# A fused recurrent and attention block: the gate sums by a triangular product, a group norm in small steps, and index queries for three token blocks

## The chip, the cores and the metric

The kernel runs on one core of a Trainium2 chip. The time is the device time of one execution in microseconds (us), and the median of several runs is compared. Engines are named as in the profile: PE is TensorE's matmul, PEld its weight load, DVE is VectorE, ACT is ScalarE, POOL is GpSimd, SP is SyncE, which issues most transfers.

## The reference

One sequence of 512 tokens, width 1024, fp32. A first block (a mixer that joins mLSTM and RWKV7, cross attention to a memory, a convolved gated feed-forward) is followed by a second one (sparse attention over the keys that an index picks, latent attention, memory attention, gated branches). Of this, the change touches three places:

```python
def mlstm_chunkwise(q, k, v, i_pre, f_pre):        # per head
    logi, logf = i_pre, jax.nn.log_sigmoid(f_pre)
    b = jnp.cumsum(logf, -1)                        # inside a chunk
    g = b[..., -1]                                  # at its end
    a = g[..., None] - b + logi
    ...                                             # running maximum m over the chunks
    d = jnp.where(causal, b[..., :, None] - b[..., None, :] + logi[..., None, :], -jnp.inf)

def standardize_heads(y, eps):                      # the RWKV output, 8 heads of 64
    mu = jnp.mean(y, -1, keepdims=True)
    var = jnp.mean(jnp.square(y - mu), -1, keepdims=True)
    return (y - mu) * lax.rsqrt(var + eps)

def dsa_attention(q, k, v, qi, ki, wi):             # topk = min(256, 512 // 4) = 128
    def one_block(args):                            # a block is 128 queries
        dots = jnp.einsum('bqhc,bsc->bhqs', qib, ki) * (IDX_DIM ** -0.5)
        index = jnp.einsum('bhqs,bqh->bqs', jax.nn.relu(dots), wib * (IDX_HEADS ** -0.5))
        index = jnp.where(causal[None], index, NEG)
        _, idx = lax.top_k(index, topk)
        valid = idx <= q_pos[None, :, None]
        ...
```

In the first block of 128 queries no query sees more than 128 keys, so the 128 best of them are all that it sees, whatever the index says.

## The kernel before, in words

All dense products are fp32 taken apart in two parts: weights come as 256 KB units by SP's DMA into `wraw` (seven buffers), ACT rounds the high part `whi` (L153), DVE takes the low part `wlo` (L156), and PE does three matmuls of 128x512 for each depth of 128 and block (hh·whi, hl·whi, hh·wlo; `dense_tok`, L271 to L282, `mmd`, L178). PSUM's eight banks are dealt by tag: mm and q two each (dense sums), p two, s and y one each.

The program is written as Python generators that yield after each small step. `woven` merges two of them by their yields' positions: the recurrence's steps are spread evenly between dense products, so that PE has something to do while a step's result passes through ACT and DVE. PE's order is fixed as it is written there; a scheduler orders DVE, ACT and POOL by priorities and what is ready, and each engine then works through its queue in that order. A matmul into bank p must wait until the reader of the bank's former content is done, wherever that reader stands in its engine's queue.

In time, the stages are: RWKV preparation up to 160 us; inverses of small triangular matrices (they use the products KR·BK, masked to `Gm` on DVE) woven with the mLSTM projections and `gates`, to 255; the RWKV chain with the mLSTM's chunks and the memory's keys, to 430; then output, cross attention and the feed-forward to 960; the second block to the end, 1601.

Three functions are touched. `gates` (L960) works on rows of 4 partitions x 512 tokens: the log-sigmoid of the forget gate, a scan for the running maximum (L976), a second scan that adds up inside chunks of 128 (L981), two subtractions and a copy that put three quantities into `um` (the tile `yt`), then four transposes on PE, and four tiny products that spread the chunk-end values over 128 partitions by a selection matrix `selX` (L357 to L361).

`rwkv_chain` steps through 16 half-chunks of 32 tokens: `tok` transposes the chunk's inputs, `solve` and `ops` (L803) make its small operators, `step` (L820) applies them. `ops` ends in additions of DR into `St` on DVE, which empty bank p. After each four half-chunks, `rwkv_out` (L868) norms 128 tokens: statistics and aggregation for eight heads (L877, L878), a reciprocal root, then two transposes and the gating. Its stages run at fixed places of the main loop (L844 to L866). In the mixer the merged sequence counts 95 steps (`CS`).

In the second block `cols` (L1626) projects a group of columns for all four token blocks and `evac` (L1638) copies them with their row scale; `index_cols` (L1672) does so for the index queries `qi`, woven with the memory attention (`memory`, L1765), and `index` (L1688) rotates them. Block 0 of `qi` is computed but not read.

Of the kernel before, what the change touches and what calls it, by code (L numbers as in the profile page):

```python
# [8 lines left out]
F32 = mybir.dt.float32  # L9
F32R = mybir.dt.float32r  # L10
I32 = mybir.dt.int32
AF = mybir.ActivationFunctionType
# [87 lines left out]
class Build:  # L100
# [234 lines left out]
    def masks(self, keep, pool):  # L335
# [11 lines left out]
        for q in range(2):  # L347
# [8 lines left out]

        selX = keep.tile([128, 512], F32, name="selX")  # L357
        nc.gpsimd.affine_select(out=selX[32:64], in_=self.one[32:64].to_broadcast([32, 512]),
                                pattern=[[-1, 4], [0, 128]], base=0, channel_multiplier=1,
                                compare_op=OP.is_equal, fill=0.0)  # L360
        self.sel4 = selX[32:36].rearrange("p (q c) -> p q c", q=4)  # L361
# [359 lines left out]
    def rwkv_chain(self, ch, TT, yT):  # L721
# [122 lines left out]
        z, st = yield from tok(0)  # L844
        yield from solve(0, z)
        yield from ops(z, st)
        late = iter(())
        for g in range(8):
            if g < 7:
                t = yield from tok(g + 1)  # L850
            yield from part(late, 1)
            yield from step(g, 0, z, st)
            if g < 7:
                yield from solve(g + 1, t[0])
            if g % 2:
# [5 lines left out]
            if g < 7:  # L861
                z, st = t
                yield from ops(z, st)
            if g % 2 == 0:
                yield from part(late, 1)
        yield from late  # L866

    def rwkv_out(self, y, b, yT):  # L868
# [91 lines left out]
    def gates(self, ml, gt):  # L960
# [3 lines left out]
        um, sg = R["yt"], R["sg"]  # L964
        g4 = lambda: self.tile(gt, [4, 512], "g4", 5)
        li = g4()
        lf = g4()
        self.act(li, um[32:36])
        self.act(lf, um[64:68])
        e = g4()  # L970
# [4 lines left out]
        m = g4()  # L975
        nc.vector.tensor_tensor_scan(m, lf, li, 0.0, op0=OP.add, op1=OP.max)  # L976
        rst128 = e
        nc.gpsimd.memset(rst128, 1.0)
        nc.gpsimd.memset(rst128.rearrange("p (c t) -> p c t", t=128)[:, :, 0:1], 0.0)
        bc = g4()  # L980
# [4 lines left out]
        ends = gt.tile([64, 2, 4], F32, name="ends")[32:36]  # L985
        nc.gpsimd.memset(ends, 0.0)
        nc.vector.tensor_copy(ends[:, 0, :], um[32:36, 127::128])
        nc.vector.tensor_copy(ends[:, 1, 1:4], m[:, 127:511:128])
        yield 0
        p = self.pt("q")  # L990
        for c in range(NB):
            self.tr(p[:, 128 * c:128 * c + 128], um[:, 128 * c:128 * c + 128])
        cl = ml.tile([128, 4, 3, 4], F32, name="cl")
# [5 lines left out]
        self.act(eb, p[:, 0:32].rearrange("p (h a c) -> p h a c", h=4, a=2))  # L999
# [457 lines left out]
    def rope(self, pool, x, heads, c0, half):  # L1457

        sh = [128, 4, heads, half]
        cos = self.cos[:, :, None, c0:c0 + half].to_broadcast(sh)  # L1460
        sin = self.sin[:, :, None, c0:c0 + half].to_broadcast(sh)
# [105 lines left out]
    def block2(self, main, late, xT, kept, out):  # L1567
# [3 lines left out]
        with tc.tile_pool(name="b2", bufs=1, reuse_waits=RW) as p2, xd as dram:  # L1571
# [54 lines left out]
            def cols(c0, n, nk=None, src=w, ks=KD, x=h, fill=None):  # L1626

                pss = [self.pm() for _ in range(NB)]
# [9 lines left out]
            def evac(pss, t, n, scaled=True):  # L1638
                for b in range(NB):
                    if scaled:  # L1640
# [31 lines left out]
            def index_cols():  # L1672
                yield from run(1536, 512, "qi", "s1", evac)
# [9 lines left out]
                for b in range(NB):  # L1683
                    self.act(ckv[:, b], pss[b][:, 0:288], AF.Copy, scale=r2[:, b:b + 1])
                    self.act(ki[:, b, 0], pss[b][:, 288:352], AF.Copy, scale=r2[:, b:b + 1])
                    self.act(wi[:, b], pss[b][:, 352:360], AF.Copy, scale=r2i[:, b:b + 1])

            def index():  # L1688
                qi, ki, wi = T["qi"], T["ki"], T["wi"]
                self.rope(p2, qi.rearrange("p b (h d) -> p b h d", h=8)[:, :, :, 0:16], 8, 0, 8)  # L1690
# [386 lines left out]
```

## Time and profile before

| | |
|---|---|
| median of 3 runs | 1605.58 us (1602.59 to 1607.35) |
| profiled execution | 1603.29 us |
| its span, from first to last instruction | 1601.4 us |
| mean granted clock of PE | 0.988 |
| busy share: PE, DVE, ACT, POOL | 97%, 68%, 47%, 6% |
| chain of waits: PE, DVE, ACT | 70%, 6%, 1% of the span |

The busy share counts instructions that overlap only once. A matmul's listed duration includes its way through the array: of a row of them each begins before the one ahead ends. The granted clock is given as a share of 2.4 GHz; half is the lower of the two levels. A square bracket at a row's end says how long the engine stood idle before it and what ended that.

### The profile page before, as it was taken

How to read it: one execution, taken by the hardware profiler on the slowest of the kernel's cores; microseconds unless marked ns; L12 is line 12 of the kernel's file. 1: busy time of each engine (PE TensorE's matmuls, PEld its weight loads, DVE VectorE, ACT ScalarE, POOL GpSimd, SP SyncE). 2: the span in 40 equal slices, each digit the busy share in tenths (PEclk: the TensorE clock that was granted, in tenths of full speed). 3: DMA queues.
4: the chain of work that ended last, by engine and by line, in shares of the span. 5: the costliest groups of instructions: out<-in, count | busy, mean ns of one | idle time of the engine just before them, and what ended most of it. 6: DMA issues, size and time to landing. Idle time of an engine off the chain costs nothing.

```text
span 1601.4 us, 23792 instructions
## 1 busy us (share of the span) xinstructions
PE 1558.0 (97%) x8515; PEld 1250.0 (78%) x8515; DVE 1091.9 (68%) x2540; ACT 752.2 (47%) x1470; POOL 94.0 (6%) x234
## 2 busy tenths in 40 slices
PE   7999899998999999999999999999999999999999
PEld 5777787787787878888888888888877778677787
DVE  6776697888756556534554578769998758755563
ACT  5645455565545435433432444446454445543431
POOL 7000402111000000000000001000000000000000
PEclk9999899999999999999999999999999999999999
DMA  7433122133534123333333334142322213224232
GB/s 256 143 66 86 41 60 53 41 107 99 159 95 142 47 86 92 99 93 98 96 95 95 91 98 113 50 120 74 90 64 67 66 53 92 67 60 125 59 93 86
DMA packets 209590, 144.84 MB, mean 90 GB/s; under 512 B 13492, under 2 KB 190787, under 8 KB 208960
## 3 DMA queue, kind: packets, MB, share of 16 engines
q1 hardware_dynamic: 208000, 141.66, 31.2%
q0 software_dynamic: 1280, 1.52, 0.4%
q8 instruction: 67, 1.10, 0.3%
q14 instruction: 51, 0.42, 0.1%
q10 hardware_dynamic: 192, 0.14, 0.0%
HBM read 134.90 MB, written 8.39 MB: 89 GB/s over the span
## 4 chain that ended last, share of the span: by engine, by line
PE 70%; DVE 6%; ACT 1%; issue 1%; DMA 1%; DVEq 0%; ACTq 0%
PE mm L178 29%; PE q L178 29%; PE p L186 3%; PE p L189 3%; PE y L186 3%; PE s L186 2%; DVE wlo L156 1%; PE s L189 1%; DVE lqk L156 1%; PE q L186 1%; DMA kvraw<-v_kept 0%; DVE m L1730 0%; DVE s L156 0%; DVE madd L1731 0%; PE mm L186 0%
## 5 line engine op out<-in xcount | busy, mean ns | idle before, releaser
L153 ACT ACTIVATE whi<-wraw 128x512 fp32r<-128x512 f32 (+2 forms) x472 | 292.6, 622 | 514.7 <-PE mm L178 253.8
L156 DVE TENSOR_TENSOR wlo<-wraw,whi 128x512 fp32r<-128x512 f32 (+2 forms) x472 | 319.5, 678 | 202.9 <-ACT whi L153 198.8
L178 PE MATMUL mm<-hh,whi 128*128 128x512 f32 (+1 forms) x680 | 252.9, 389 | 1.2 <-ACT hh L153 0.9
L178 PE MATMUL mm<-hh,wlo 128*128 128x512 f32 (+1 forms) x616 | 237.1, 385 | 0.0
L178 PE MATMUL mm<-hl,whi 128*128 128x512 f32 x552 | 219.3, 397 | 0.0
L178 PEld LDWEIGHTS mm<-hh,whi 128*128 128x128 f32 x680 | 124.5, 190 | 25.8 <-issue 2.7
L178 PE MATMUL q<-hl,whi 128*128 128x512 f32 x352 | 139.4, 396 | 0.0
L178 PE MATMUL q<-hh,whi 128*128 128x512 f32 x352 | 139.0, 395 | 0.0
L178 PE MATMUL q<-hh,wlo 128*128 128x512 f32 x352 | 139.0, 395 | 0.0
L178 PEld LDWEIGHTS mm<-hh,wlo 128*128 128x128 f32 x616 | 116.9, 190 | 22.1 <-issue 0.5
L178 PEld LDWEIGHTS mm<-hl,whi 128*128 128x128 f32 x552 | 105.0, 190 | 20.0 <-issue 1.4
L178 PEld LDWEIGHTS q<-hl,whi 128*128 128x128 f32 x352 | 66.4, 189 | 14.7 <-issue 1.6
L178 PEld LDWEIGHTS q<-hh,wlo 128*128 128x128 f32 x352 | 66.4, 189 | 14.3 <-issue 1.0
L178 PEld LDWEIGHTS q<-hh,whi 128*128 128x128 f32 x352 | 66.5, 189 | 14.0 <-issue 0.9
L178 PE MATMUL q<-whi,hh 128*128 128x512 f32 (+2 forms) x176 | 69.0, 394 | 0.0
L178 PE MATMUL mm<-whi,hh 128*128 128x512 f32 (+2 forms) x176 | 68.7, 392 | 0.0
L178 PE MATMUL mm<-wlo,hh 128*128 128x512 f32 (+2 forms) x160 | 61.6, 385 | 0.0
L178 PE MATMUL q<-wlo,hh 128*128 128x512 f32 (+2 forms) x160 | 61.5, 385 | 0.0
L178 PE MATMUL mm<-whi,hl 128*128 128x512 f32 (+2 forms) x144 | 55.3, 384 | 0.0
L178 PE MATMUL q<-whi,hl 128*128 128x512 f32 (+2 forms) x144 | 55.3, 384 | 0.0
L153 ACT ACTIVATE at_sm<-at_sm,at_mx 128x128 f32<-128x128 f32 (+3 forms) x64 | 35.8, 559 | 41.2 <-DVE at_mx L1538 40.8
L174 DVE SCALAR_TENSOR_TENSOR fy<-fc,vcols,fy 128x512 f32<-128x512 f32 x44 | 33.0, 751 | 8.9 <-ACT fy L153 8.2
(702 smaller groups left out, 3167.2 us busy)
## 6 DMA issues: line engine op xcount, KB each, us to landing
wraw<-in_w_in_dram SPq DMA_DIRECT2D x172, 256.0 KB, 2.8
wraw<-in_f_up_dram SPq DMA_DIRECT2D x88, 256.0 KB, 2.9
wraw<-in_f_down_dram SPq DMA_DIRECT2D x40, 256.0 KB, 2.7
wraw<-in_x_wkv_dram SPq DMA_DIRECT2D x32, 256.0 KB, 3.0
wraw<-in_w_out_dram SPq DMA_DIRECT2D x32, 256.0 KB, 2.7
wraw<-in_w_branch_dram SPq DMA_DIRECT2D x24, 256.0 KB, 2.7
wraw<-in_w_mem_kv_dram SPq DMA_DIRECT2D x16, 256.0 KB, 4.7
wraw<-in_x_wq_dram SPq DMA_DIRECT2D x16, 256.0 KB, 2.8
```

Of the source, the lines that this page charges most:

```text
L153: self.pin("a", self.nc.scalar.activation(out, in_, func, **kw))
L156: self.pin("v", self.nc.vector.tensor_tensor(out, a, b, op=op))
L174: self.pin("v", self.nc.vector.scalar_tensor_tensor(out, a, s, b, op0=op0, op1=op1))
L178: ins = self.nc.tensor.matmul(out, lhsT=a, rhs=b, start=start, stop=stop)
L186: self.pin("p", self.nc.tensor.matmul(out, lhsT=a, rhs=b, start=start, stop=stop))
L189: self.pin("p", self.nc.tensor.transpose(out, in_, self.ident if ident is None else ident))
```

## The change

**Gates.** Only the maximum's scan stays on the rows, and it writes straight into `um`. The transposes follow. The sum inside a chunk is then a product with a triangle of ones (`upto`, 128x128) on the transposed 128x16 columns, two small subtractions follow, and the chunk-end values are spread by a product with a matrix whose last row is ones (`last`). `selX` is gone; POOL builds the two matrices.

**Group norm.** `rwkv_out` yields after four heads' statistics, after eight, and after the reciprocal root. The chain's main loop is a generator of its own, and behind each third of its steps one step of the oldest unfinished norm runs.

**Index queries.** Block 0 of `qi` and `wi` is neither projected nor copied, and the rotation runs over blocks 1 to 3.

```diff
     def dense_tok(self, pss, w, x, ks, first, last, cols):
-        order = [(a, t) for a in range(n) for t in range(len(pss))]
+        order = [(a, t) for a in range(n) for t in range(len(pss)) if pss[t] is not None]
...
     def rwkv_chain
-        z, st = yield from tok(0)
-        yield from solve(0, z)
-        yield from ops(z, st)
-        late = iter(())
-        for g in range(8):
-            if g < 7:
-                t = yield from tok(g + 1)
-            yield from part(late, 1)
-            yield from step(g, 0, z, st)
-            if g < 7:
-                yield from solve(g + 1, t[0])
-            if g % 2:
-                yield from late
-            yield from step(g, 1, z, st)
-            if g % 2:
-                late = self.rwkv_out(ys[g // 2 % 2], g // 2, yT)
-                yield from part(late, 1)
...
+        lates = []
+        def main():
...
+                yield from step(g, 1, z, st)
+                if g % 2:
+                    lates.append(self.rwkv_out(ys[g // 2 % 2], g // 2, yT))
...
+        for n, at in enumerate(main()):
+            yield at
+            if n % 3 == 2 and lates and next(lates[0], "end") == "end":
+                lates.pop(0)
+        for late in lates:
+            yield from late

     def rwkv_out(self, y, b, yT):
         for h in range(8):
             nc.vector.bn_stats(st[:, h], ynv[:, h])
             nc.vector.bn_aggr(ag[:, h], st[:, h])
+            if h == 3:
+                yield 0
+        yield 0
         var = rt("gvar", (128, 8), 1)
         self.ts(var, ag[:, :, 1], 64e-5, None, OP.add)
         r = self.rsqrt(ch, var, 8)
+        yield 0
...
     def gates(self, ml, gt):
-        nc.vector.tensor_tensor_scan(m, lf, li, 0.0, op0=OP.add, op1=OP.max)
...
-        nc.vector.tensor_tensor_scan(bc, rst128, lf, 0.0, op0=OP.mult, op1=OP.add)
-        self.sub(um[32:36], bc, m)
-        self.sub(um[64:68], li, bc)
-        nc.vector.tensor_copy(um[96:100], m)
...
-        nc.vector.tensor_copy(ends[:, 0, :], um[32:36, 127::128])
-        nc.vector.tensor_copy(ends[:, 1, 1:4], m[:, 127:511:128])
+        nc.vector.tensor_tensor_scan(um[96:100], lf, li, 0.0, op0=OP.add, op1=OP.max)
+        upto = gt.tile([128, 128], F32, name="upto")
+        nc.gpsimd.affine_select(out=upto, ...)
+        last = gt.tile([128, 128], F32, name="last")
+        nc.gpsimd.affine_select(out=last, ...)
         yield 0
         p = self.pt("q")
         for c in range(NB):
             self.tr(p[:, 128 * c:128 * c + 128], um[:, 128 * c:128 * c + 128])
-        self.act(cl, p.rearrange("p (c q x) -> p c q x", c=4, q=4)[:, :, 1:4, 0:4])
+        self.act(raw, pv[:, :, 1:3, 0:4].rearrange("p c q x -> p q c x"))
+        self.act(cl[:, :, 2, :], pv[:, :, 3, 0:4])
         p = self.pt("q")
-        for hd in range(4):
-            self.mm(p[:, 8 * hd:8 * hd + 8], self.sel4[:, hd, :], ends.rearrange("p a c -> p (a c)"))
+        bc = p[:, 0:16].rearrange("p (c x) -> p c x", c=4)
+        self.mm(bc, upto, raw[:, 1])
+        self.sub(cl[:, :, 0, :], bc, cl[:, :, 2, :])
+        self.sub(cl[:, :, 1, :], raw[:, 0], bc)
+        yield 0
+        p = self.pt("q")
+        pv = p[:, 0:48].rearrange("p (c q x) -> p c q x", c=4, q=3)
+        self.mm(pv, last, cl)
...
+        self.act(ebv[:, 0], pv[:, :, 0])
+        self.act(ebv[:, 1, 1:4], pv[:, 0:3, 2])
...
             def index_cols():
-                yield from run(1536, 512, "qi", "s1", evac)
+                yield from run(1536, 512, "qi", "s1", evac, b0=1)
```

The change moves instructions on DVE and PE. First DVE's queue at the gates; `g` are the tiles of four rows, `yt` is `um`, and the `p` that `Gm` reads is the bank that PE wants next. Before:

```order
L156 TENSOR_TENSOR Gm_613<-p_1760,gmask 128x512
L174 SCALAR_TENSOR_TENSOR g_1688<-g_1688,g_1691 4x512
L156 TENSOR_TENSOR wlo_1838<-wraw_1837,whi_1839 128x512
L976 SCALAR_TENSOR_TENSOR g_1696<-g_1688,g_1687 4x512
L981 SCALAR_TENSOR_TENSOR g_1700<-g_1691,g_1688 4x512
L984 COPY yt<-g_1696 4x512
L156 TENSOR_TENSOR yt<-g_1700,g_1696 4x512
L156 TENSOR_TENSOR yt<-g_1687,g_1700 4x512
L987 COPY ends<-yt 4x4
L988 COPY ends<-g_1696 4x3
L174 SCALAR_TENSOR_TENSOR q_1730<-mc_1727,vcols_573,q_1730 128x512
L156 TENSOR_TENSOR wlo_1977<-wraw_1976,whi_1978 128x512
```

And now, up to the next two masked products:

```order
L174 SCALAR_TENSOR_TENSOR yt<-yt,g_1686 4x512
L156 TENSOR_TENSOR Gm_611<-p_1748,gmask 128x512
L973 SCALAR_TENSOR_TENSOR yt<-yt,g_1685 4x512
L156 TENSOR_TENSOR wlo_1826<-wraw_1825,whi_1827 128x512
L174 SCALAR_TENSOR_TENSOR q_1718<-mc_1715,vcols_573,q_1718 128x512
L156 TENSOR_TENSOR Gm_611<-p_1772,gmask 128x512
L174 SCALAR_TENSOR_TENSOR q_1718<-mc_1715,vcols_573,q_1718 128x512 x2
L156 TENSOR_TENSOR wlo_1970<-wraw_1969,whi_1971 128x512
L156 TENSOR_TENSOR Gm_611<-p_1799,gmask 128x512
```

Between two masked products there stood two scans, three operations on rows and two tiny copies; one scan is left.

PE's order at the same place. Before, the transposes of `um` and the four products with `selX` stand between a product of the inverses and the dense ones:

```order
L186 MATMUL p_1882<-KR_607,BK_608 64x64 x16
L189 MATMUL q_1900<-ident,yt 128x128 x4
L186 MATMUL q_1907<-ends,selX 128x8 x4
L178 MATMUL mm_1843<-hh_80,whi_1839 128x512
L178 MATMUL mm_1843<-hl_81,whi_1839 128x512
```

Now:

```order
L186 MATMUL p_1870<-KR_605,BK_606 64x64 x16
L189 MATMUL q_1888<-ident,yt 128x128 x4
L186 MATMUL q_1897<-graw,upto 128x16
L186 MATMUL q_1901<-cl,last 128x48
L178 MATMUL mm_1831<-hh_80,whi_1827 128x512
L178 MATMUL mm_1831<-hl_81,whi_1827 128x512
```

Two products stand in place of four, the first behind ACT's copy `graw` of the transposes, the second behind DVE's `cl`, and no dense product stands between them.

Last, DVE's queue in the chain at the first group norm (`gst`, `gag` are its statistics; `rs_` and `Dm` belong to the mLSTM's norm). Before, the additions into `St` stand behind the last statistics:

```order
L156 TENSOR_TENSOR rs_y_3352<-rs_y_3352,rd_3336 128x4
L878 BN_AGGR gag_3374<-gst_3373 128x2 x2
L171 TENSOR_SCALAR Dm_2946<-nt_3115,mag_3339,rs_y_3352 128x128 x4
L877 BN_STATS gst_3373<-sg 128x6 x2
L878 BN_AGGR gag_3374<-gst_3373 128x2
L156 TENSOR_TENSOR St_3152<-p_3429,DR 64x384
L878 BN_AGGR gag_3374<-gst_3373 128x2
L156 TENSOR_TENSOR St_3153<-p_3429,DR 64x384
L169 TENSOR_SCALAR gvar_3391<-gag_3374 128x8
L156 TENSOR_TENSOR sg<-sg,gag_3374 128x512
```

Now four of them stand ahead of the first:

```order
L156 TENSOR_TENSOR St_3145<-p_3366,DR 64x384
L174 SCALAR_TENSOR_TENSOR rs_y_3345<-rs_t_3347,rs_y_3345 128x4
L156 TENSOR_TENSOR St_3146<-p_3366,DR 64x384
L156 TENSOR_TENSOR rs_t_3347<-rs_y_3345 128x4
L156 TENSOR_TENSOR St_3145<-p_3395,DR 64x384
L156 TENSOR_TENSOR rs_t_3347<-rs_t_3347,rs_h_3346 128x4
L156 TENSOR_TENSOR St_3146<-p_3395,DR 64x384
L174 SCALAR_TENSOR_TENSOR rs_y_3345<-rs_t_3347,rs_y_3345 128x4
L874 BN_STATS gst_3428<-sg 128x6
```

The statistics now begin after these additions, mixed with the same steps of the mLSTM's norm, and the copies of `Z` come behind their first lot.

## Rows read from the trace of the kernel before

**Rows 1.** The page's busy times: us (share of the span) xinstructions.

```profile
PE 1558.0 (97%) x8515; PEld 1250.0 (78%) x8515; DVE 1091.9 (68%) x2540; ACT 752.2 (47%) x1470; POOL 94.0 (6%) x234
```

**Rows 2.** Windows: us; busy PE, PEld, DVE, ACT, POOL; PEclk, DMA share, GB/s.

```profile
150.00:200.00 50.00, 45.62 (x456) 37.13 (x455) 35.26 (x55) 24.88 (x46) 17.56 (x15) 0.90 0.20 48
304.00:440.00 136.00, 122.88 (x1220) 103.66 (x1219) 113.97 (x330) 73.27 (x150) 19.66 (x34) 0.97 0.38 113
1015.00:1065.00 50.00, 49.81 (x292) 41.86 (x292) 36.44 (x88) 19.80 (x52) 0.00 (x0) 1.00 0.25 77
1080.00:1240.00 160.00, 158.89 (x802) 126.00 (x801) 149.57 (x431) 86.55 (x197) 3.40 (x11) 1.00 0.28 73
```

**Rows 3.** Timeline of PE at the gates: start, us, instruction [idle before <-releaser].

```profile
177.99 1.97 PE L186 MATMUL p<-KR,BK 64*64 64x64 f32 x32 [4.29 <-DVE Gm L156]
...
185.12 1.05 PE L186 MATMUL q<-ends,selX 4*128 4x8 f32 x8
```

**Rows 4.** Timeline of DVE at the gates.

```profile
170.52 2.22 DVE L981 TENSOR_TENSOR_SCAN g<-g,g 4x512 f32<-4x512 f32 x1
172.77 1.33 DVE L984 COPY yt<-g 4x512 f32<-4x512 f32 x1
174.13 1.40 DVE L156 TENSOR_TENSOR yt<-g,g 4x512 f32<-4x512 f32 x2
...
177.16 1.28 DVE L156 TENSOR_TENSOR Gm<-p,gmask 128x512 f32<-128x512 f32 x2
```

**Rows 5.** Windows behind PE's waits; columns as in rows 2.

```profile
178.00:184.00 6.00, 6.00 (x60) 4.88 (x62) 1.79 (x4) 1.23 (x2) 0.00 (x0) 0.56 0.19 46
196.00:204.00 8.00, 8.00 (x59) 6.92 (x58) 3.56 (x13) 3.32 (x7) 3.19 (x2) 0.57 0.13 33
312.00:316.00 4.00, 2.84 (x11) 2.60 (x12) 3.77 (x13) 1.19 (x3) 1.22 (x3) 0.62 0.01 2
320.00:332.00 12.00, 9.45 (x106) 8.03 (x106) 9.16 (x19) 7.77 (x17) 1.28 (x2) 1.00 0.38 109
408.00:412.00 4.00, 4.00 (x20) 3.38 (x19) 2.12 (x4) 2.77 (x7) 0.00 (x0) 0.57 0.71 252
```

**Rows 6.** Timeline of ACT at the gates.

```profile
173.85 0.63 ACT L153 ACTIVATE xt<-bonus 128x512 f32<-128x512 f32 x1 [3.42 <-POOL w L948]
...
174.90 0.58 ACT L153 ACTIVATE vT<-mm 128x512 f32<-128x512 f32 x1
175.50 1.28 ACT L153 ACT_TABLE_LOAD   x1
176.79 0.63 ACT L153 ACTIVATE th<-q 128x512 f32<-128x512 f32 x1
...
185.23 0.21 ACT L153 ACTIVATE cl<-q 128x48 f32<-128x48 f32 x1 [1.32 <-PE q L189]
```

**Rows 7.** Timeline of POOL at the gates.

```profile
167.76 0.51 POOL L978 MEMSET g<- 4x512 f32 x1 [4.51 <-DVE g L174]
...
171.73 2.08 POOL L948 TENSOR_TENSOR w<-xt,w 32x512 fp32r<-32x512 f32 x1
```

**Rows 8.** POOL's select of 128x128 on tile causT: ns min/median/max, first and last start.

```profile
L366 POOL TENSOR_SCALAR_AFFINE_SELECT causT<-zero x1: 292/292/292, 23.4 to 23.4; 128x128 f32<-128x128 f32 x1
```

**Rows 9.** PE's waits in 304–440: line <- releaser: us, times, longest.

```profile
PE p L189 <- DVE sg L156: 3.6, 2, 2.6
PE p L189 <- DVE gvar L169: 3.1, 3, 2.1
PE p L189 <- DVE mag L1122: 2.1, 1, 2.1
```

**Rows 10.** Statistics on DVE in 304–440: count | busy us, mean ns | idle before.

```profile
L878 DVE BATCH_NORM_AGGREGATE gag<-gst 128x2 f32<-128x6 f32 x32 | 5.0, 167 | 0.0
L877 DVE BATCH_NORM_STATS2 gst<-sg 128x6 f32<-128x64 f32 x16 | 3.1, 207 | 0.0
```

**Rows 11.** The chain of waits in the second block: start, us, what.

```profile
1006.33 5.44 PE mm L178 x24
```

More of the change, by code (lines that the diff above doesn't have):

```diff
@@ L355, in masks @@
         nc.gpsimd.memset(self.hsel[64:128, 1:2], 1.0)
[L357 to L361, printed above, removed]
         zero = pool.tile([128, 128], F32, name="zero")
@@ L842, in step @@
                 yield 0
-        z, st = yield from tok(0)
-        yield from solve(0, z)
-        yield from ops(z, st)
-        late = iter(())
-        for g in range(8):
-            if g < 7:
-                t = yield from tok(g + 1)
-            yield from part(late, 1)
-            yield from step(g, 0, z, st)
-            if g < 7:
-                yield from solve(g + 1, t[0])
-            if g % 2:
-                yield from late
-            yield from step(g, 1, z, st)
-            if g % 2:
-                late = self.rwkv_out(ys[g // 2 % 2], g // 2, yT)
-                yield from part(late, 1)
[L861 to L866, printed above, removed]
+        lates = []
+        def main():
+            z, st = yield from tok(0)
+            yield from solve(0, z)
+            yield from ops(z, st)
+            for g in range(8):
+                if g < 7:
+                    t = yield from tok(g + 1)
+                yield from step(g, 0, z, st)
+                if g < 7:
+                    yield from solve(g + 1, t[0])
+                yield from step(g, 1, z, st)
+                if g % 2:
+                    lates.append(self.rwkv_out(ys[g // 2 % 2], g // 2, yT))
+                if g < 7:
+                    z, st = t
+                    yield from ops(z, st)
+        for n, at in enumerate(main()):
[4 more added lines that the diff above has]
+            yield from late
     def rwkv_out(self, y, b, yT):
@@ L962, in gates @@
         sc = 0.25 / math.sqrt(128.0)
[L964 to L967, printed above, removed]
+        um = R["yt"]
+        li, e = (self.tile(gt, [128, 512], "g4", 2)[64:68] for _ in range(2))
+        lf = um[64:68]
         self.act(li, um[32:36])
-        self.act(lf, um[64:68])
-        e = g4()
         self.act(e, lf, AF.Abs)
@@ L974, in gates @@
         self.stt(lf, lf, 0.0, e, OP.min, OP.subtract)
-        m = g4()
-        nc.vector.tensor_tensor_scan(m, lf, li, 0.0, op0=OP.add, op1=OP.max)
[L977 to L980, printed above, removed]
-        nc.vector.tensor_tensor_scan(bc, rst128, lf, 0.0, op0=OP.mult, op1=OP.add)
-        self.sub(um[32:36], bc, m)
-        self.sub(um[64:68], li, bc)
-        nc.vector.tensor_copy(um[96:100], m)
-        ends = gt.tile([64, 2, 4], F32, name="ends")[32:36]
-        nc.gpsimd.memset(ends, 0.0)
-        nc.vector.tensor_copy(ends[:, 0, :], um[32:36, 127::128])
-        nc.vector.tensor_copy(ends[:, 1, 1:4], m[:, 127:511:128])
+        nc.vector.tensor_tensor_scan(um[96:100], lf, li, 0.0, op0=OP.add, op1=OP.max)
+        upto = gt.tile([128, 128], F32, name="upto")
+        nc.gpsimd.affine_select(out=upto, in_=self.one.to_broadcast([128, 128]), pattern=[[1, 128]], base=0,
+                                channel_multiplier=-1, compare_op=OP.is_ge, fill=0.0)
+        last = gt.tile([128, 128], F32, name="last")
+        nc.gpsimd.affine_select(out=last, in_=self.one.to_broadcast([128, 128]), pattern=[[0, 128]], base=-127,
+                                channel_multiplier=1, compare_op=OP.is_equal, fill=0.0)
         yield 0
@@ L1455, in tables, with rope @@
         self.cos, self.sin = cos, sin
[L1457 to L1461, printed above, removed]
+    def rope(self, pool, x, heads, c0, half, b0=0):
+        sh = [128, NB - b0, heads, half]
+        cos = self.cos[:, b0:, None, c0:c0 + half].to_broadcast(sh)
+        sin = self.sin[:, b0:, None, c0:c0 + half].to_broadcast(sh)
         x1, x2 = x[:, :, :, 0:half], x[:, :, :, half:2 * half]
@@ L1624, in sums, with cols @@
                 self.ts(r2i, r2, 8.0 ** -0.5)
-            def cols(c0, n, nk=None, src=w, ks=KD, x=h, fill=None):
-                pss = [self.pm() for _ in range(NB)]
+            def cols(c0, n, nk=None, src=w, ks=KD, x=h, fill=None, b0=0):
+                pss = [None] * b0 + [self.pm() for _ in range(b0, NB)]
                 nk = nk or 1024 // n
@@ L1639, in evac @@
                 for b in range(NB):
+                    if pss[b] is None:
+                        continue
                     if scaled:
```

10 lines of the change are left out of this document (7 added, 3 removed).

## The prediction

> **What bounds the kernel now.** I read the line of busy times first: PE is busy for 97% of the span and DVE for 68% [rows 1]. So the time is PE's, and an edit is worth what it takes from PE's work, from PE's idle time, or from the stretches in which PE runs at half its clock. Then I read the windows of the stages that the diff touches [rows 2]: PE idles 4.4 us in 150–200 and 13.1 us in 304–440 (the RWKV chain, where DVE is busy for 114 of 136 us), but 0.2 us in 1015–1065, where the index queries are projected. In 1080–1240 (the top-k search) PE and DVE are both nearly full: 158.9 and 149.6 of 160 us. The timelines and waits then say which instruction ended PE's idle time, and the clock windows what followed.
>
> All sums are made against the profiled execution: 1603.3 us, a span of 1601.4 and 1.9 around it, which I leave as it is. The median of the runs is 1605.6, so 2.3 is added at the end.
>
> **Gates, about 175 us.** PE waits 4.29 us at 173.7 to 177.99 for the second mask product of DVE (Gm) [rows 3]. In DVE's queue that product stands behind the second scan (2.22), the copy of the maxima (1.33), two subtractions (1.40) and two tiny copies [rows 4], 5.3 us in all. All of these go, or become subtractions on 128x16 columns after PE's transposes, so Gm can be done at 172.5 instead of 177.8, and PE, which comes for it at 173.7, need not wait: −4.3. The time after the wait also shows: in 178–184 the granted clock is 0.56, that is, mostly the lower of the two levels (1.2 of 2.4 GHz); at full clock the six us of PE work would take 3.4: −2.6 [rows 5]. PE ran at 1.00 until it stood still; if it no longer stands still, the fall has no cause that I see. The eight tiny products with selX take 1.05 us [rows 3] and are replaced by one of 16 and one of 48 columns: −0.5.
>
> What is late next? First the eviction of vT on ACT. Before, it stands at 174.90, ahead of a table load (1.28) and th (0.63) [rows 6]; now it is queued behind both, and ACT gets to them only after the copy of the bonus, which waits for POOL's subtraction on w (2.08) [rows 6, 7]. POOL loses two fills (0.5 and less) and ends w at 173.2; the bonus and a weight split take 1.05 (the time from 173.85 to 174.90), then 1.28, 0.63 and vT's own 0.58: 176.7. PE arrives at 173.7 + 1.0 (half of 1.97, at full clock) + 0.7 (three products) = 175.4 to 175.5: +1.2. What stands behind that wait on PE is everything, since its order is fixed. Second, PE must now wait in line for ACT's copy of the transposed sums and DVE's subtractions between its two small products. The nearest row for the copy is 0.21 us, begun 0.04 after the transposes [rows 6]; two DVE operations of this size about 0.3. With both engines free that is 0.6, with one other instruction ahead on each (0.63 on ACT, 0.7 on DVE) 1.9. I take 0.7, near the free case, since ACT had idled 1.3 us before that copy. Building the two triangles costs POOL two selects of 0.29 [rows 8], before anyone needs them. Sum: −4.3 −2.6 −0.5 +1.2 +0.7 = **−5.5**; bounds −7.4 (no new wait) and −1.7 (the second wait at 1.9, and the clock falls all the same). The selX fill, near the program's start, is long done when it is read: 0.
>
> **Group norm in the chain.** Six waits of PE in 304–440 belong to it [rows 9]: 3.6 us (two, by name for sg), 3.1 (three, gvar), 2.1 (one, mag), together 8.8 of the 13.1 us of idle time. The releasers are not what PE needs: its next transposes go to a bank that becomes free when DVE has added the block to St, and that addition is queued behind the norm's statistics. One block's eight statistics and eight aggregations are 1.6 and 1.3 us [rows 10] (half of the one row's sum, a quarter of the other's), mixed with as much of the mLSTM's norm. In the new order four St additions come before the first of these statistics, and the statistics come in two lots of four heads. The work itself stays: DVE has the same 114 us in 136 us, so some of the delay moves to the next reader, the Z copies behind the lot (its head lot is 1.5 us and the mLSTM's share about as much). So I take half of the waits: −4.4. Of the half-clock stretches 312–316 (0.62) and 408–412 (0.57) [rows 5], which cost 1.5 and 1.7 us and both follow a wait of over 2 us, I take two thirds: −2.1. Sum **−6.5**; the bounds are −12.0 (all waits and both stretches) and +2.0 (DVE's queue is only reshuffled, one wait of 2.1 like that for mag is added). The steps issue no DMA. Since the chain's steps end some thirty products earlier, the loads of x for the next stage stand four weight loads earlier on SP; the DMA share there is 0.71 [rows 5], so I cost this at nothing; it is weights that hide it, four to seven loads ahead.
>
> **Index queries.** Block 0 loses three products on each of eight k: 24 products of 128x512. The chain of waits shows 24 of these in 5.44 us [rows 11], 0.227 each, at clock 1.00. In 1015–1065 PE has no idle time in which they could hide [rows 2], so −5.4. The scaled eviction of one block leaves ACT (19.8 of 50 us) and a quarter of six rope operations DVE (36.4): nothing on the path. Against it: the memory attention is woven between these products and now has nine in place of twelve to cover each turn of its softmax; I give back 1.0 for that. Sum **−4.5**, bounds −5.4 and 0 (all is lost when DVE's full stretch at 1080–1240 comes up).
>
> Total: −5.5 −6.5 −4.5 = −16.5, so 1586.8 for the profiled execution and **1589** against the median.
>
> **Rivals.**
> - *The gates' wait comes back under other names* (0.13): vT, the copy and the subtractions and the fall of the clock eat most of it and the saving is 1.7. For it: ACT's wait of 3.42 for POOL [rows 6] is untouched. Against: DVE is relieved of 5 us just there. −12.7: 1593.
> - *The group norm's waits only move* (0.19): the Z copies are late instead, saving 1.0. For it: DVE's 84% [rows 2]. Against: half of what PE waited for stood behind work that PE does not need. −11.0: 1594.5.
> - *More goes* (0.11): all waits and both half-clock stretches of the chain (12.0), the whole 5.4, and the stretch 196–204 at 0.57 [rows 5], 3.4, which I otherwise leave. −26.3: 1579.
> - *The index saving is swallowed* (0.07) by DVE's 149.6 of 160 us [rows 2]. For it: PE can't run ahead of the top-k. Against: PE is full there as well, and DVE can start earlier by as much. −12: 1593.5.
> - *Slower* (0.06): the norm in small steps gives PE more, shorter waits in the chain, and they hold its clock at the lower level. Work done at 1.2 GHz takes twice its time, so of each us there half is lost. The gains elsewhere (5.5, 4.5, and 4.4 of waits) are 14.4 us, so it decides from 29 us at the lower level; with 50 us, +25 −14.4 = +10.6: 1616. Against it stands a row: 320–332 has 2.55 us of idle time in 12, in waits of at most 1.0, at clock 1.00 [rows 5]. The Trainium skill speaks for this rival (TensorE: Matmul & The Clock Gate, A second HAM failure mode: psum-queue depth-cycling): frequent small idles between groups of matmuls, as banks are cycled, make the clock swing between its levels. By that rule this time would be likely; by the row it is not, and I go by the row.
> - Two or more of these losses together, or a stall that I don't see, leave it where it was (0.08).
>
> **How the numbers follow.** The forecast itself has 0.36, with 1583 to 1595 as its own range: gates −3 to −7, norm −3 to −10, index −3 to −5.4, not all at one end. The range 1576 to 1602 takes in the first four rivals and the lighter part of the last; it leaves out the slower case and most of no change. A difference below 0.3% (4.8 us) can't be told from none here. Faster: 0.36 + 0.13 + 0.19 + 0.11 + 0.07 = 0.86; within 0.3% 0.08; slower 0.06.
>
> **What would show it.** Right: no wait of over 1.5 us before the Gm-fed products near 175 and a clock of 1.00 in the six us behind; PE's waits named sg, gvar and mag in the chain below 4.4 us, and at least one of its two half-clock stretches gone; 72 products for the index queries, and the stages behind the gates, the chain and the projection ending about 5.5, 12 and 16.5 us earlier. Wrong: a wait on vT or on the new products as long as the old one, Z copies as releasers of several us in the chain, a granted clock below 0.95 over the chain, or stages after the projection that take longer by what it saved.

## The result and the profile after

The changed kernel takes 1589.28 us (median of 4 runs, 1588.84 to 1592.04), the kernel before 1604.09 (4 runs, 1600.29 to 1607.35): a ratio of 0.9906, with a 95% interval of 0.9883 to 0.9929. The forecast was 1589. It was made from a median of 1605.6 of three runs and a drop of 16.5 us; a fourth run brought that median to 1604.1, and the drop is 14.8. The span of the profiled execution fell from 1601.4 to 1587.2 us. First its line of busy times, where PE has lost 11.0 us of work or listed overlap [rows 1]:

```profile
PE 1547.0 (97%) x8487; PEld 1241.5 (78%) x8487; DVE 1088.2 (69%) x2536; ACT 751.2 (47%) x1469; POOL 93.6 (6%) x233
```

Where the 14.2 us of the span went is read by setting equal PE instructions of both traces against each other and taking the difference of their start times:

| PE reaches | after minus before, us | difference in the stretch | forecast |
|---|---|---|---|
| dense work at 40 us, behind the wait for km | +2.2 | +2.2 | 0 |
| 206, behind the gates | −2.8 | −5.0 | −5.5 |
| 307, before the first group norm | −4.8 | −2.0 | 0 |
| 500, behind the chain | −7.8 | −3.0 | −6.5 |
| 950, the second block | −8.6 | −0.8 | 0 |
| 1240, behind the index queries | −14.3 | −5.7 | −4.5 |
| the end | −14.2 | +0.1 | 0 |

The row at 307 is a step of the chain; 816 dense products stand ahead of it in place of 819, so 0.7 us of its −2.0 is work that comes later, and the chain's own share is −3.7 rather than −3.0. The stages behind the gates, the chain and the projection end 2.8, 7.8 and 14.3 us earlier, where 5.5, 12 and 16.5 were forecast.

The windows that answer to [rows 2], with the last two set 10 to 15 us earlier (columns as there):

```profile
150.00:200.00 50.00, 48.24 (x465) 38.53 (x464) 35.55 (x56) 25.53 (x48) 16.94 (x12) 0.93 0.22 54
304.00:440.00 136.00, 125.64 (x1216) 106.06 (x1215) 111.26 (x327) 74.76 (x151) 20.48 (x33) 0.99 0.38 116
1000.00:1050.00 50.00, 49.78 (x298) 42.02 (x298) 37.99 (x92) 22.93 (x59) 0.00 (x0) 1.00 0.25 74
1070.00:1225.00 155.00, 153.89 (x771) 121.71 (x771) 146.26 (x423) 83.93 (x190) 3.39 (x11) 1.00 0.27 73
```

PE's idle time in 304–440 fell from 13.1 to 10.4 us only, while the stages with the index stayed full: there the work itself is less. At the gates, PE's timeline (start, us, instruction, idle time before it) now has three short waits in place of the one of 4.29 [rows 3]:

```profile
178.43 0.66 PE L189 MATMUL q<-ident,vT 128*128 128x128 f32 x4 [0.55 <-ACT vT L153]
...
181.82 0.37 PE L186 MATMUL q<-graw,upto 128*128 128x16 f32 x2 [0.38 <-ACT cl L153]
182.69 0.39 PE L186 MATMUL q<-cl,last 128*128 128x48 f32 x2 [0.50 <-DVE cl L156]
```

The windows behind them, to be held against [rows 5], show that the clock stays at 1.00 in 178–184, where it was 0.56, and falls right after in this trace. The third row answers to 196–204, where it was 0.57:

```profile
178.00:184.00 6.00, 4.69 (x56) 3.54 (x58) 3.74 (x11) 2.66 (x11) 0.00 (x0) 1.00 0.36 87
184.00:190.00 6.00, 6.00 (x74) 4.71 (x71) 1.58 (x4) 0.20 (x2) 1.14 (x1) 0.72 0.01 3
194.00:202.00 8.00, 8.00 (x52) 6.87 (x51) 4.18 (x14) 3.41 (x6) 3.09 (x2) 0.79 0.05 6
```

And PE's waits in 304–440 (line, releaser: us, times, longest). None of the names of [rows 9] is left, but others stand there:

```profile
PE p L189 <- DVE St L156: 2.6, 2, 2.2
PE p L189 <- DVE yt L156: 2.5, 1, 2.5
PE p L186 <- DVE Z L766: 2.2, 3, 1.0
PE p L186 <- DVE Z L801: 1.9, 2, 1.1
PE p L189 <- DVE Z L766: 0.8, 1, 0.8
```

### The profile page after: what moved, and what is told of

Read it like the earlier page. It is cut to its first block, busy times and chain, and to the rows that moved or that the text cites. A ratio compares the mean times of both kernels' runs of the same rounds, so it can differ in the third digit from the quotient of the medians.

```text
span 1587.2 us, 23736 instructions
## 1 busy us (share of the span) xinstructions
PE 1547.0 (97%) x8487; PEld 1241.5 (78%) x8487; DVE 1088.2 (69%) x2536; ACT 751.2 (47%) x1469; POOL 93.6 (6%) x233
## 4 chain that ended last, share of the span: by engine, by line
PE 70%; DVE 6%; issue 1%; ACT 1%; DMA 1%; DVEq 0%; ACTq 0%
PE mm L178 30%; PE q L178 27%; PE p L186 3%; PE p L189 3%; PE y L186 3%; PE s L186 2%; DVE wlo L156 1%; PE s L189 1%; DVE lqk L156 1%; PE q L186 1%; DMA kvraw<-v_kept 1%; DVE m L1739 0%; DVE s L156 0%; DVE madd L1740 0%; PE mm L186 0%
## 5 line engine op out<-in xcount | busy, mean ns | idle before, releaser
L178 PE MATMUL mm<-hh,whi 128*128 128x512 f32 (+1 forms) x744 | 278.0, 389 | 0.0
L178 PE MATMUL mm<-hh,wlo 128*128 128x512 f32 (+1 forms) x680 | 262.3, 386 | 0.0
L178 PE MATMUL mm<-hl,whi 128*128 128x512 f32 x616 | 245.2, 398 | 0.0
L178 PEld LDWEIGHTS mm<-hl,whi 128*128 128x128 f32 x616 | 116.8, 190 | 23.2 <-issue 2.8
L178 PE MATMUL q<-hh,whi 128*128 128x512 f32 x288 | 113.7, 395 | 0.0
L178 PE MATMUL q<-hl,whi 128*128 128x512 f32 x288 | 113.1, 393 | 0.0
L178 PE MATMUL q<-hh,wlo 128*128 128x512 f32 x288 | 112.9, 392 | 0.0
L178 PEld LDWEIGHTS q<-hh,whi 128*128 128x128 f32 x288 | 54.5, 189 | 11.6 <-issue 0.7
L178 PEld LDWEIGHTS q<-hh,wlo 128*128 128x128 f32 x288 | 54.4, 189 | 11.3
L178 PEld LDWEIGHTS q<-hl,whi 128*128 128x128 f32 x288 | 54.4, 189 | 11.0 <-issue 0.2
```

The source lines that it names most:

```text
L178: ins = self.nc.tensor.matmul(out, lhsT=a, rhs=b, start=start, stop=stop)
```

## The experiments

Each kernel was run in five rounds against the kernel before; ratios are to that one, with 95% intervals. The changed kernel's own interval, 0.9883 to 0.9929, is wide, so a run on top of it says little by its ratio alone. Four questions were open: whether the parts add up, where the +2.2 us at the start came from, why the norm gave half of its term, and what the clock does.

**1. The gates alone** (`gates` and the selX fill as in the change, the rest as before).

```diff
-        nc.gpsimd.affine_select(out=selX[32:64], ...)
...
-        nc.vector.tensor_tensor_scan(bc, rst128, lf, 0.0, op0=OP.mult, op1=OP.add)
...
+        self.mm(bc, upto, raw[:, 1])
...
+        self.mm(pv, last, cl)
```

> Only the gates' part of the change on the kernel before (the selX fill is gone with it). In the trace of the whole change PE is 2.5 us later than before at 30 us (it waits 4.03 us instead of 1.85 for ACT's km) and gains 5.3 us between 173 and 204. Theory S: the later start belongs to this part, since POOL, without the selX fill (0.81 us), comes earlier to its own subtraction (lwl) and disturbs DVE's reciprocal root: km is waited for again by about 4 us, and the net is -5.3 + 2.3 = -3 us, ratio 0.998. Rival C: the late start is chance of one execution: no longer wait for km, -5.3 us, ratio 0.9967. In both: no wait for Gm near 175, three waits of together about 1.4 us (vT, graw, cl), and one stretch of some 2.7 us at half clock behind them that costs 1.3.

Measured: 0.9965 (0.9952 to 0.9977), 1599.03 us, that is −5.6 us. PE's waits at the gates are 0.55, 0.38 and 0.51, as in the changed kernel, but the half-clock stretch that was expected behind them did not come; one stands at 190–196 instead:

```profile
181.75 0.39 PE L186 MATMUL q<-cl,last 128*128 128x48 f32 x2 [0.51 <-DVE cl L156]
```

```profile
184.00:190.00 6.00, 6.00 (x63) 4.74 (x64) 3.37 (x4) 1.12 (x2) 3.60 (x2) 1.00 0.02 4
190.00:196.00 6.00, 6.00 (x59) 5.58 (x59) 1.97 (x5) 2.40 (x4) 4.64 (x3) 0.79 0.17 43
```

The wait for km is 1.67 us, not longer than before, though PE is still 1.1 us late at 40 us. Theory S's 0.998 lies outside the interval; the rival's 0.9967 lies inside.

**2. The group norm alone** (the three new yields and `main()` with a step of the norm behind each third of its own).

```diff
+        for n, at in enumerate(main()):
+            yield at
+            if n % 3 == 2 and lates and next(lates[0], "end") == "end":
...
```

> Only the group norm's part on the kernel before. Theory M (waits move): the waits for sg, gvar and mag (8.8 us) are gone, about 10 us of others stand in 304 to 440 (St, Z, the last block's yt), both half-clock stretches are gone (3.2 us), one comes at the end of the chain; net -3 us in the chain, ratio 0.998. Rival (the sum on record): -6.5, ratio 0.996. The start is as before: km waited for by about 1.9 us if theory S of the gates' run holds.

Measured: 0.9978 (0.9966 to 0.9989), 1601.54 us: −3.5 us. In its trace PE gains 4.3 us between 307 and 437 (5.0 with the 0.7 of work put off). The waits for sg, gvar and mag are gone, and 9.4 us of others for St, Z and yt stand there. The half-clock stretch that was expected at the end of the chain did not come; one stands near 331 us. Theory M holds for the waits and the size; 0.996 lies outside the interval.

**3. The index queries alone.**

```diff
...
-                yield from run(1536, 512, "qi", "s1", evac)
+                yield from run(1536, 512, "qi", "s1", evac, b0=1)
...
```

> Only the index queries for blocks 1 to 3 on the kernel before. Theory F (full price): 24 products by 0.227 us and nothing given back, -5.4 to -5.7 us, ratio 0.9965. Rival (the sum on record): -4.5, 0.9972. Rival: swallowed by DVE's full stretch behind it, 0, 1.000. The start as before.

Measured: 0.9969 (0.9958 to 0.9981), 1599.66 us: −5.0 us. The runs can't tell −4.5 from −5.4, but the trace can: PE is 1.7 us late at 1010 and 4.0 early at 1240, −5.7, as in the whole change (runs 1 and 2, without the edit, lose 0.5 and 0.7 us there). Nothing is given back to the softmax or to DVE's full stretch. The three parts come to −5.6 −3.5 −5.0 = −14.1 us, the whole change to 0.94% of 1604, −15.1: they add up within the intervals.

Its start, which should have been as before, was late (PE's timeline, the only row of its wait for km):

```profile
29.93 0.50 PE L178 MATMUL mm<-whi,m2h 128*128 128x512 f32 x1 [4.07 <-ACT km L153]
```

**4. The whole change with the fill back.**

```diff
+        selX = keep.tile([128, 512], F32, name="selX")
+        nc.gpsimd.affine_select(out=selX[32:64], in_=self.one[32:64].to_broadcast([32, 512]), ...)
```

> The whole change with the selX fill put back on POOL at its old place; nothing reads it. Theory S: km is waited for by about 1.9 us again and all that follows comes 2.3 us earlier than in the changed kernel: -16.5 us against the kernel before, ratio 0.990. Rival C (chance of one execution): no difference from the changed kernel, ratio 0.9906 to 0.9912, and the wait for km is as long in some kernels with the fill as without it.

Measured: 0.9902 (0.9882 to 0.9922), 1588.39 us; no difference from the change (0.9906). Its wait for km happened to be 1.19 us:

```profile
26.89 0.50 PE L178 MATMUL mm<-whi,m2h 128*128 128x512 f32 x1 [1.19 <-ACT km L153]
```

So the kernels with the fill have shown 1.85, 1.22, 4.07 and 1.19 us for this wait, those without it 4.03 and 1.67, and in runs 5 to 11 from 1.28 to 3.90: theory S is dead. The wait varies by up to 2.9 us from one execution to the next, and the +2.2 of the table is that.

**5. Dense products between the gates' small ones.**

```diff
         self.act(cl[:, :, 2, :], pv[:, :, 3, 0:4])
+        yield 0
         p = self.pt("q")
...
-    ... part(lstm, 12), gates, part(lstm, GS), ...
+    ... part(lstm, 12), part(gates, 1), part(lstm, 1), part(gates, 1), part(lstm, 1), gates, part(lstm, GS - 2), ...
```

> The changed kernel, with three dense products between the transposes of um and the product with upto, and three between that and the product with last. In the changed kernel PE waits 0.38 us for ACT's cl and 0.50 for DVE's cl there, and runs 2.7 us at half clock right behind (184.9 to 187.6), at a cost of 1.3. Theory W (the clock fell for these idle times): both waits and the half-clock stretch go, -2.2 us against the changed kernel, ratio to the kernel before about 0.989. Rival T (it fell for the run of small products and transposes there, which are the same): the waits go, the stretch stays, -0.9 us, 0.990.

Measured: 0.9898 (0.9881 to 0.9914), 1588.66 us: no difference that the runs can tell. In the trace both waits are gone, and 184–190 has a clock of 1.00. Another half-clock stretch stands six us later:

```profile
184.00:190.00 6.00, 5.88 (x75) 5.00 (x74) 5.32 (x9) 2.45 (x8) 4.83 (x3) 1.00 0.01 3
190.00:196.00 6.00, 6.00 (x49) 5.21 (x49) 3.38 (x8) 1.79 (x3) 3.44 (x2) 0.72 0.16 44
```

This decides nothing between the theories: runs 1, 4, 6, 7 and 8 kept both waits (0.38 and 0.50 or 0.51), and in each of them the clock stayed at 1.00 for the eight us behind as well. The stretch at 184–190 stood in the changed kernel's one trace only. Between 40 and 262 us PE gains 6.7 us on the kernel before, against 5.1 in the changed kernel and 6.2 in run 1; near 265 us 0.4 of it are lost again, where the changed kernel gained 1.2 (told of below). The runs do not confirm the gain.

**6. The chain's steps wider.**

```diff
-PS, LS, CS, XS = 16, 75, 95, 188
+PS, LS, CS, XS = 16, 75, 80, 188
```

> The changed kernel with the chain's steps set wider (80 in place of 95 per unit of the woven sequence). The norm's steps no longer count as steps, so the main steps stand 105/88 closer among the dense products than before; 80 gives them their former distance. Theory P (the density of the chain's steps on DVE causes the waits that are left, 10.3 us in the chain): they fall to about 6, -3 to -4 us against the changed kernel, ratio to the kernel before about 0.988. Rival D (what stands ahead in DVE's queue at each norm causes them, whatever the distance): the same 10 us, the chain ends later with fewer dense products behind it, 0 to +2 us, 0.9906 to 0.992.

Measured: 0.9882 (0.9866 to 0.9897), 1586.55 us. PE's waits in 304–440 (as above), where the long ones for St and yt are down to 0.6 and 0.4:

```profile
PE mm L178 <- DVE hh L156: 1.2, 1, 1.2
PE p L186 <- DVE Z L766: 1.1, 3, 0.4
...
PE p L189 <- DVE St L156: 0.6, 2, 0.4
...
PE p L189 <- DVE yt L156: 0.4, 1, 0.4
```

All of them come to 7.5 us, against 10.2 in the changed kernel. That is for theory P, with a smaller step than it gave. Two things go against a simple reading. At 80 the steps do not have their former distance but a wider one: between the first and the last products of St with Z stand dense products worth 261 of 512 columns before, 237 in the changed kernel and 282 here. And the chain has a longer half-clock stretch, near 309 to 319 us (windows of the changed kernel and of this run):

```profile
308.00:324.00 16.00, 14.54 (x177) 11.94 (x174) 15.48 (x54) 9.01 (x19) 1.95 (x5) 1.00 0.33 96
```

```profile
304.00:440.00 136.00, 128.49 (x1205) 107.92 (x1206) 112.60 (x306) 77.68 (x156) 18.44 (x33) 0.96 0.38 115
308.00:324.00 16.00, 14.28 (x137) 13.18 (x138) 12.24 (x33) 8.12 (x18) 0.52 (x2) 0.68 0.40 116
```

The loss of 5.1 us (16 times 0.32) stands at the same place in runs 9 and 10, which also have 80. What causes it was not tested.

**7. No reciprocal root in the group norm** (the variance is the factor; this part of the computation is left out).

```diff
-        r = self.rsqrt(ch, var, 8)
+        r = var
```

> The changed kernel without the reciprocal root of the RWKV group norm: the variance itself is the factor, so twelve small DVE operations per norm, which follow one another and take 3 us in all with what comes between, are left out. Theory D (PE's remaining waits stand behind this chain on DVE): the wait for St (2.18) and the last one for yt (2.47, with its half-clock stretch of 1.7) shrink by most of their length, -3 to -5 us against the changed kernel, ratio about 0.988. Theory P (density of steps): DVE loses 2 of 111 us there and the waits stay within 1 us of 10.3; 0 to -1, 0.990.

Measured: 0.9875 (0.9858 to 0.9892), 1585.80 us. The wait for yt is gone, St's longest is 1.5, and between 307 and 437 PE gains 9.2 us on the kernel before instead of 3.0. Of these 6.2 us 3.4 are idle time and 1.7 the half-clock stretch. The longest waits in 304–440:

```profile
PE p L186 <- DVE Z L766: 2.2, 3, 1.0
PE p L189 <- DVE St L156: 1.9, 3, 1.5
PE p L189 <- DVE Z L766: 1.2, 1, 1.2
PE p L186 <- DVE Z L801: 0.7, 1, 0.7
```

For yt theory D holds. In the changed kernel DVE ends the root with the first of these rows, only then makes yt, and PE stands still for it:

```profile
418.70 0.17 DVE L174 SCALAR_TENSOR_TENSOR rs_y<-rs_t,rs_y 128x8 f32<-128x8 f32 x1
418.90 0.69 DVE L156 TENSOR_TENSOR yt<-yt,rs_y 128x512 f32<-128x512 f32 x1
```

```profile
419.64 0.66 PE L189 MATMUL p<-ident,yt 128*128 128x128 f32 x4 [2.47 <-DVE yt L156]
```

For the other waits the run doesn't separate the theories. Theory P's number was worked out with 2 us less work on DVE; in the changed kernel's trace the four roots' 48 operations have 7.4 us of DVE's time, so leaving them out also makes its queue less dense.

**8. The norm's two wide operations on POOL.**

```diff
-        self.sub(ynv, ynv, ag[:, :, 0:1].to_broadcast([128, 8, 64]))
-        self.mul(ynv, ynv, r[:, :, None].to_broadcast([128, 8, 64]))
+        nc.gpsimd.tensor_tensor(ynv, ynv, ag[:, :, 0:1].to_broadcast([128, 8, 64]), op=OP.subtract)
+        nc.gpsimd.tensor_tensor(ynv, ynv, r[:, :, None].to_broadcast([128, 8, 64]), op=OP.mult)
```

> The changed kernel with the group norm's subtraction and multiplication (two operations of 128x512 per norm, 0.68 us each on DVE) moved to POOL, which is busy for 20 of 136 us there. Theory D: DVE's queue is shorter by 1.36 us at each norm and the waits for St and Z fall by 2 to 3 us in all, though the last norm's yt comes later (POOL took 1.3 to 2.1 us for such an operation near 170): -1 to -2 us, ratio about 0.990. Rival X (POOL's operations hold up DVE's while they run, as far as the trace lets one think so): DVE's own operations there get longer and nothing is gained, 0 to +3 us, 0.991 to 0.9925.

Measured: 0.9880 (0.9865 to 0.9894), 1585.65 us. In the trace St's waits fall to 1.2 us, and the last norm's rises:

```profile
PE p L189 <- POOL yt L884: 3.3, 1, 3.3
...
PE p L189 <- DVE St L156: 1.2, 3, 0.7
```

Its chain gains only 0.3 us on the changed kernel. The rest of its trace's lead lies where the instructions are the same: 0.9 at the start, 1.3 at the gates and 1.5 in the clock near 265 (below). So the ratio is no evidence for POOL. What rival X names is seen too: three short operations of DVE, which mostly take 0.15 to 0.17 us, took 0.89 to 1.02 beside POOL's and ended within 0.03 us of them. The first of them, and the same one in the changed kernel:

```profile
311.07 1.05 POOL L883 TENSOR_TENSOR sg<-sg,gag 128x512 f32<-128x512 f32 x1 [5.96 <-DVE gag L875]
```

```profile
311.14 1.01 DVE L212 TENSOR_SCALAR rs_i<-gvar 128x8 int32<-128x8 int32 x1
```

```profile
316.11 0.15 DVE L212 TENSOR_SCALAR rs_i<-gvar 128x8 int32<-128x8 int32 x1
```

**9 to 11. The pieces together**, all on one chip: 9 has the spread products and the wider steps (edits 5 and 6), 10 has in addition POOL for the first three norms, 11 is 10 with the steps at 95 again.

```diff
+        eng = nc.vector if b == 3 else nc.gpsimd
+        eng.tensor_tensor(ynv, ynv, ag[:, :, 0:1].to_broadcast([128, 8, 64]), op=OP.subtract)
+        eng.tensor_tensor(ynv, ynv, r[:, :, None].to_broadcast([128, 8, 64]), op=OP.mult)
```

> The changed kernel with both the dense products between the gates' small ones and the chain's steps at 80. If the two gains add (0.9 us of waits and the half-clock stretch behind them; about 2.4 us in the chain), some 4 us less than the changed kernel, ratio to the kernel before about 0.987. If the gates' gain is given back, as in the run with it alone, by the half-clock stretch near 265 us that comes and goes between executions with the same waits, the ratio is that of the steps at 80 alone, 0.988.

> The same, with the group norm's subtraction and multiplication on POOL for the first three of the four norms, and on DVE for the last, for which PE waited 3.29 us when POOL did them. Theory D (DVE's queue): the St wait is under 1 us, the last yt wait under 0.5; another -1 to -2 us, ratio about 0.986. Rival (the wider steps have taken these waits already): no difference from the run without POOL, 0.987.

> As the one before, but with the chain's steps at 95 again. Theory D: St's wait falls from 2.18 to 0.7, yt's stays at 2.5 with its half-clock stretch, -1 to -2 us against the changed kernel with the spread products, ratio about 0.9885. If the distance of the steps is what counts, it is over 2 us slower than with 80.

| | median of runs | ratio |
|---|---|---|
| 9, spread, steps at 80 | 1585.78 (1583.98 to 1586.30) | 0.9887 (0.9874 to 0.9901) |
| 10, and POOL for three norms | 1585.93 (1583.51 to 1586.56) | 0.9888 (0.9874 to 0.9901) |
| 11, spread, POOL, steps at 95 | 1589.17 (1588.35 to 1590.56) | 0.9909 (0.9895 to 0.9923) |

The distance of the steps is worth 3.2 us (10 against 11, whose runs do not overlap). POOL adds nothing: 10 equals 9, though its waits for St and yt are down to 0.2 and 0.3 us, and with the steps at 95, 11 (0.9909) is no faster than run 5 (0.9898). Against the rounds of 6, the spread products add nothing either; run 9's rival gave the number, but not the reason, since its trace has a clock of 1.00 near 265. So the best version found is the change with its steps at 80, 17 to 19 us below the kernel before (runs 9 and 6).

**The clock near 265.** In the kernels with the steps at 95 the chain's first steps have the same three waits there. Before, and in run 4 (PE's timeline):

```profile
263.51 1.08 PE L186 MATMUL p<-rgu,TT 32*32 32x128 f32 x32 [0.88 <-ACT whi L153]
266.71 0.38 PE L186 MATMUL p<-St,Z 32*64 32x96 f32 x4 [0.91 <-ACT Z L153]
267.35 0.70 PE L186 MATMUL p<-St,Z 32*64 32x96 f32 x10 [0.26 <-DVE Z L807]
```

```profile
255.48 1.08 PE L186 MATMUL p<-rgu,TT 32*32 32x128 f32 x32 [0.91 <-ACT whi L153]
258.69 0.38 PE L186 MATMUL p<-St,Z 32*64 32x96 f32 x4 [0.93 <-ACT Z L153]
259.32 0.70 PE L186 MATMUL p<-St,Z 32*64 32x96 f32 x10 [0.26 <-DVE Z L806]
```

The eight us that begin six us after the first of these rows (windows; the clock is the third number from the end), of before, of the changed kernel and of run 4:

```profile
269.51:277.51 8.00, 7.80 (x43) 6.17 (x40) 3.18 (x8) 3.01 (x6) 2.15 (x5) 0.63 0.02 4
```

```profile
266.62:274.62 8.00, 7.48 (x59) 5.89 (x59) 4.03 (x9) 3.56 (x7) 2.16 (x5) 0.79 0.13 30
```

```profile
261.48:269.48 8.00, 7.47 (x80) 5.89 (x77) 4.88 (x11) 4.19 (x8) 2.16 (x5) 1.00 0.13 33
```

The same waits, and a clock of 0.63, 0.79 or 1.00: in the eight us that is from 3.0 us to nothing. In runs 2 and 3 it was 0.63 and 0.65, in 5 and 7 0.68 and 0.70, in 11 0.79, in 1 and 8 1.00; in 6, 9 and 10, which have their steps elsewhere, 1.00. The three kernels with the old gates lie at 0.63 to 0.65. Those with the new ones spread from 0.68 to 1.00, and of these the changed kernel and runs 4, 7 and 8 have the same instructions up to there but for one fill. What decides it was not settled.

## Why the prediction was right

The time came out as forecast, in part by luck: the drop was 14.8 us where 16.5 was forecast, and the median of the kernel before came out 1.5 us lower than the one it was reckoned from. Of the three terms two had about the right size, and the third was about half.

**What bounds the kernel.** Right: what came off PE's work (index) showed in full, and what came off its idle time (gates) nearly so.

**Gates, −5.5.** Right in the mechanism, and in the sum: −5.0 in the trace, −5.6 alone (−6.1 in that trace). Gm was no longer waited for. The two new waits were 0.55 for vT, where I had 1.2, and 0.38 + 0.50 for the small products, where I had 0.7. The clock's part was right by luck in this trace. It fell anyway for a while behind the small products: 0.72 in 184–190 costs 1.7 us (6 times 0.28), against 2.6 in 178–184 before. And the stretch 196–204, which I had left alone, gave up to 1.7 us of its 3.4 (0.79 in 194–202 now). The first is no price of the new waits, since in five runs with the same waits the clock stayed at 1.00 behind them.

The queue ahead of Gm was perhaps not all of the gates' own making. Its two scans of 4x512 took 2.36 and 2.22 us while POOL worked on `rgl`, `x` and `w` (168.2 to 173.8 [rows 7]). At 65 us in the same trace, with POOL idle, a scan of 128x512 took about half of that (DVE's timeline of before):

```profile
64.85 1.23 DVE L619 TENSOR_TENSOR_SCAN rt<-rst,rt 128x512 f32<-128x512 f32 x1
```

No run moved POOL's work away from there, so whether that alone would have shortened the wait stays open.

**Group norm, −6.5.** The step that failed is "so I take half of the waits: −4.4" with "two thirds" of the half-clock stretches, −2.1. The six waits of 8.8 us did all go, but the idle time of the chain fell by 2.7 us only (13.1 to 10.4), since waits for St, yt and Z of 10.0 us took their place (these names had 1.8 before). Both half-clock stretches went too in this trace, and a new one came behind the wait for yt (window of the changed kernel):

```profile
420.00:424.00 4.00, 4.00 (x15) 3.25 (x14) 1.84 (x3) 2.62 (x6) 0.00 (x0) 0.57 0.30 73
```

It costs 1.7 us, so the clock's part was −1.5. Together that is −4.2; the trace shows −3.7 with the 0.7 us of work put off, the run of this part alone −3.5. The clock's part is a matter of one execution: in run 4, whose chain has the same instructions and the same waits, the clock over the chain is 0.96, no better than the 0.97 before:

```profile
304.00:440.00 136.00, 126.86 (x1193) 107.84 (x1194) 107.66 (x304) 74.63 (x150) 18.31 (x28) 0.96 0.39 117
```

The prediction's sentence that "some of the delay moves to the next reader" was right, and its amount too small: the sign named there as wrong, "Z copies as releasers of several us", did come, with 4.9 us. The mechanism that I did not weigh is that the norm's steps no longer count in the woven sequence. I saw that the chain would end some thirty products earlier, but asked only what that does to the loads. The main steps then stand closer among the dense products (237 in place of 261, run 6), DVE's queue gets denser, and the root's dependent operations stand ahead of yt. Runs 10 and 11 show the first by their times, run 6 by its waits; run 7 shows the second for yt. How the wait for St divides between the two stays open. The rival "the waits only move" had the better mechanism; its size (−1.0) was too small.

**Index queries, −4.5.** The 1.0 that I gave back to the softmax was not lost: −5.7 in two traces, −5.0 by the runs alone, against 5.4 for 24 products at their rate. The swallowing by DVE's full stretch did not come.

**What was not in the sum.** The start (+2.2) and, of the stretch to 307 (−2.0), the 1.3 near 265 vary between executions with the same instructions, by the runs above; the other 0.7 is the work put off. The −0.8 between 500 and 950 is mostly a wait for the softmax of the cross attention that was 3.72 us before and 2.93 after; runs 1 to 3 had 3.14, 3.20 and 3.02 without an edit there. It stays open.

**Rivals.** The slower case did not come: with ten waits of up to 2.5 us in the chain, the clock there was 0.99 in the changed kernel and 0.96 in run 4, after 0.97. What the lower level cost there was 1.7 to 5.1 us, not the 25 of this rival. Here the row of before was the better guide than the rule on frequent small idles that the prediction quotes from the Trainium skill (TensorE: Matmul & The Clock Gate, A second HAM failure mode: psum-queue depth-cycling).

## What to carry to other kernels

An engine that works through its queue in order releases a buffer only when it gets there, so look at what stands ahead of the releasing instruction, not at the instruction that the wait names; and a long chain of tiny dependent operations there can count for more than a wide one. When small steps are moved into others' places in a woven order, check whether the density of the rest has changed: here setting the steps wider again was worth 3.2 us. And a single pair of traces carries a few us of chance: take the sizes of parts from runs of each part alone.

## What the runs showed of the hardware

The same short waits (0.9, 0.9 and 0.3 us) were followed by a granted clock of 0.79 in the changed kernel and 1.00 in run 4, whose instructions up to there are the same but for one fill, and by 0.63 in the kernel before: up to 3.0 us in one place. The Trainium skill says of one kernel measured several times that the number of slow matmuls at its start changed from run to run (TensorE: Matmul & The Clock Gate, Part 1: The HAM clock gate); these traces show a change of that kind in the middle of a kernel. PE's wait at the start for ACT's km was between 1.19 and 4.07 us in executions whose instructions there are the same but for one fill, and that fill did not decide it. Short operations of DVE of 128x4 to 128x8 took 0.89 to 1.02 us, where they mostly take 0.15 to 0.17, when one of POOL's of 128x512 ran beside them (run 8), while additions of 64x384 from a PSUM bank kept their 0.55. Scans over 512 columns took 2.22 to 2.36 us beside POOL and 1.23 without it; that POOL is the cause was not tested apart from this.
